# In the scan of a hybrid encoder block, ScalarE and VectorE keep the order of the program, and the splits of operands are spread over the background's pieces

## The chip, the cores and the metric

One core of a Trainium2 chip runs the kernel. The metric is the device time of one execution in microseconds (us); less is better. The kernel before takes 2295.72 us (median of three runs, 2294.54 to 2297.85).

Five engines work side by side, each on its own list of instructions: TensorE (PE in the profile; PEld is its loading of weights), VectorE (DVE), ScalarE (ACT), GpSimd (POOL) and SyncE (SP). Here SP issues nearly all the DMA transfers. An instruction that needs another engine's result waits for it, and what stands behind it on the same engine waits too.

## What is computed

The block takes 1024 tokens of width 1024 and 16 meta tokens. Everything is float32. Cut to what matters here:

```python
u = rmsnorm(hs) @ w_in                 # 1024 -> 9280: g_val, g_gate, z, xs, B, C, dt_f, dt_b, gate_conv, gate_ssm
y_conv = silu(layernorm(dwconv31(g_val * sigmoid(g_gate)))) @ conv_out_w
xs, B, C = silu(dwconv7(xs, B, C))
# SSD scan, chunks of 128, 4 groups of 8 heads, head width 64, state 128, both directions
y = ssd(xs, dt_f, a_f, B, C) + rev(ssd(rev(xs), rev(dt_b), a_b, rev(B), rev(C))) + d * xs
v = y * silu(z);  v = v * rsqrt(mean over each group of v * v) * ssm_norm_w
y_ssm = v @ ssm_out_w
hs = hs + (sigmoid(gate_conv) * y_conv + sigmoid(gate_ssm) * y_ssm) @ w_o
hs = hs + (silu(h @ w_gate) * (h @ w_up)) @ w_down        # h = rmsnorm(hs)
out = rmsnorm(hs)[:, 16:]
```

Inside a chunk the scan gives, for each head, a part from the chunk itself (a 128 x 128 matrix of decays times C B^T, applied to x), a part from the state that enters from the left, and a part from the state that enters from the right.

## The kernel before, in words

**Precision.** The large matmuls run on float32 numbers that are cut in two: a high part rounded to a shorter format (names ending in h) and the remainder (ending in l). A product is then three matmuls: high by high, high by low, low by high. So each operand has a *split*: one ScalarE instruction writes the high part, one VectorE or GpSimd instruction writes the remainder. Weights are split in `load_w`: SP loads half a block into `wraw` (two buffers), ScalarE casts it into `wh` (L138), VectorE or GpSimd subtracts into `wl` (L139).

**Stages.** Norm and projection of dt and z; projection of the rest with the two convolutions on VectorE; the *scan* (690 to 1265 us of the profile); then the output products, the merge, and the feed-forward part.

**The scan.** For each of four groups g there is first a backward pass (`backward(g)`, nine chunks from the right, three steps each: transpose x, transpose B, carry the state `s_b`, which is written to DRAM), and then a forward pass over eight chunks (class `Chunk`). The loop over 33 rounds does, in round f, parts of three chunks at once: loading and scores of the next one, outputs of the current one, norm and store of the last one, and up to six steps of the next group's backward pass. A string of letters is the order:

```python
SEQ = "LsDbS0NO5t3e4Pb7eT1VCeM62b"
```

L is `load` of the next chunk: TensorE forms C B^T in tile `cb`; VectorE masks it twice (`cb`, L777 and L778); `weigh` scales it by dt into `gg` (four ScalarE instructions, L788, then four of VectorE, L790); `split_small` splits C into `cch` and `ccl` (L691, L692). D is `outputs` of the current chunk: `split_over` splits the state from the right into `sbh` (ScalarE, L685) and, in place, `s_bl` (VectorE, L686); eight small matmuls `yd`; x times d (L834), added to yd (L835). b is a step of the backward pass. S and T are the scores: matmuls `ss`, exponential into `e` on ScalarE, times gg on VectorE. N, P and V belong to the last chunk: squares (L866), scaling by the norm (L870), transposes and store (L877, L878). O is `off_diag`: one matmul with the state from the left, and three with `sbh` and `s_bl`. C carries the state, M transposes and gates.

**The background.** Digits in the string are places at which pieces of other products are put in, to keep TensorE busy: `step_bg(n)` adds n to an account and runs one piece per whole unit, on average 3.3 pieces per round. A piece is six or nine matmuls of 128 x 512, and three pieces make an output, which ScalarE copies out of its PSUM bank (`w`, L553 for the gates, L656 for `s0`). In the chunk loop the pieces have one bank, `mm`. The background is eight blocks of gate weights (96 pieces) and then half of the product with ssm_out_w (`s0`, 48 pieces), whose moving operand is the normed rows of groups 0 and 1: `load_vn(0)` reads 16 tiles of 256 KB back from DRAM through `wraw` and splits them into `oph` and `opl` (L622, L623).

**Who sets the order.** The program's text gives every instruction a priority, and a scheduler lays out each engine's list with estimates of its own, so that an instruction may come ahead of others that were written earlier. For TensorE this is switched off in the scan: `tie` makes each matmul and transpose depend on the one written before it, without a semaphore, while `strict[0]` is true. ScalarE, VectorE, GpSimd and SP are laid out by the scheduler.

Of the kernel before, what the change touches and what calls it, by code (L numbers as in the profile page):

```python
# [8 lines left out]
F32 = mybir.dt.float32  # L9
F32R = mybir.dt.float32r  # L10
AF = mybir.ActivationFunctionType
ALU = mybir.AluOpType
# [3 lines left out]
P = 128  # L16
D = 1024
KC = D // P
# [39 lines left out]
def tile_hybrid_block(  # L58
# [4 lines left out]
    w_o, norm_ffn, w_gate, w_up, w_down, norm_final, out,  # L63
):
    nc = tc.nc
    V, S, GP, PE, SP = nc.vector, nc.scalar, nc.gpsimd, nc.tensor, nc.sync
    x = x[0]
    out = out[0]

# [2 lines left out]
    wts = ctx.enter_context(tc.tile_pool(name="wts", bufs=2))  # L72
# [13 lines left out]
    d_vn = [dram.tile([P, 4, T], F32, name=f"d_vn{g}") for g in range(G)]  # L86
# [34 lines left out]

    plan = []
    ready = []

    def load_w(view, lo):

        a, b = view.shape[1], view.shape[2]
        wh = wts.tile([P, 2048], F32R, name="wh", tag="wh")
        wl = wts.tile([P, 2048], F32R, name="wl", tag="wl")
        h3 = wh[:, : a * b].rearrange("p (a b) -> p a b", b=b)  # L130
        l3 = wl[:, : a * b].rearrange("p (a b) -> p a b", b=b)
        st = a // 2
        for i in range(2):
            raw = wts.tile([P, 1024], F32, name="wraw", tag="wraw", bufs=2)
            r3 = raw[:, : st * b].rearrange("p (a b) -> p a b", b=b)
            SP.dma_start(out=r3, in_=view[:, i * st:(i + 1) * st, :])
            sl = slice(i * st, (i + 1) * st)
            S.copy(out=h3[:, sl], in_=r3)  # L138
            (V if lo[i] == "v" else GP).tensor_tensor(out=l3[:, sl], in0=r3, in1=h3[:, sl].bitcast(F32), op=ALU.subtract)  # L139
        return h3, l3  # L140

    def next_w(key):

        while plan and len(ready) < 2:
            k, view, lo = plan.pop(0)
            ready.append((k, load_w(view, lo)))
        k, w = ready.pop(0)
        assert k == key, (k, key)
        return w
# [32 lines left out]
    plan_down(NFF // 2 - 1)  # L182

    last_mm = [None]
    strict = [False]

    def tie(mm):

        if strict[0]:
            tc.add_manual_dep(mm.ins, last_mm[0].ins.name,  # L190
                              mybir.DependencyInfo(mybir.DependencyClass.NoSync, mybir.DependencyReason.DATA),
                              reason="order")
        last_mm[0] = mm

    def matmul(out_, **kw):
        tie(PE.matmul(out_, **kw))  # L196

    def transpose(out_, in_, ident_):
        tie(PE.transpose(out_, in_, ident_))

    def mm3_parts(ps, wh, wl, oph, opl, parts):

        K = len(wh)
        for k in range(K):
            for i, (a, b) in enumerate(((wh[k], oph[k]), (wh[k], opl[k]), (wl[k], oph[k]))):
                matmul(ps, lhsT=a, rhs=b, start=(k == 0 and i == 0), stop=(k == K - 1 and i == 2))
            if k + 1 in parts:
                yield
# [8 lines left out]
    R_NM, R_NF, R_CB, R_LG, R_LB, R_SB, R_SN = 0, 8, 16, 24, 32, 40, 64  # L217
# [15 lines left out]
    def prm(r, i):  # L233
        return pr[:, r + i:r + i + 1]
# [369 lines left out]
    def op_tile():  # L604
        h = opp_box[0].tile([P, 512], F32R, name="oph", tag="oph")
        l = opp_box[0].tile([P, 512], F32R, name="opl", tag="opl")
        return h, l
# [4 lines left out]

    def load_vn(kh):

        op = []
        for hh in range(2):
            for k in range(KC):
                raw = wts.tile([P, 1024], F32, name="wraw", tag="wraw", bufs=2)[:, :512]
                SP.dma_start(out=raw, in_=d_vn[2 * kh + k // 4][:, k % 4, hh * 512:(hh + 1) * 512])
                h, l = op_tile()  # L620
                w = prm(R_SN, KC * kh + k)
                S.activation(out=h, in_=raw, func=AF.Copy, scale=w)  # L622
                V.scalar_tensor_tensor(out=l, in0=raw, scalar=w, in1=h.bitcast(F32), op0=ALU.mult, op1=ALU.subtract)  # L623
                op.append((h, l))
        return op

    def gemm(op, key, ps_of, parts=()):

        for b in range(4):
            wh, wl = next_w(f"{key}{b}")  # L630
            for hh in range(2):
                for j in range(2):
                    js = slice(j * P, (j + 1) * P)
                    ps = ps_of()
                    yield from mm3_parts(ps, [wh[:, k, js] for k in range(KC)], [wl[:, k, js] for k in range(KC)],
                                         [t[0] for t in op[hh * KC:(hh + 1) * KC]],
                                         [t[1] for t in op[hh * KC:(hh + 1) * KC]], parts)
                    yield 2 * b + j, hh, ps

    def background():  # L640
        for k, i in BGP:
            if k == "z":
                yield from z_block(i, sd, ps_bg, 2)
            else:
                yield from gate_block(k, i, d_gc if k == "gc" else d_gs, sd, ps_bg)
        hn_ctx.close()
        opp_box.append(ctx.enter_context(tc.tile_pool(name="ops", bufs=16, side="right")))
        op = load_vn(0)
        yield
        for done in gemm(op, "s0", ps_bg, PARTS):  # L650
            if done is None:
                yield
                continue
            i, hh, ps = done
            pt = sd.tile([P, 512], F32, name="w512", tag="w512", bufs=2)
            S.copy(out=pt, in_=ps)  # L656
            SP.dma_start(out=d_p[i, :, hh * 512:(hh + 1) * 512], in_=pt)
            yield

    ps_bg = lambda: pb(next(bg_ring[0]))  # L660
    bg = background()
    bg_acc = [0.0]
    strict[0] = True

    def step_bg(n):
        bg_acc[0] += n
        while bg_acc[0] >= 1:
            bg_acc[0] -= 1
            next(bg, None)

    def hbc(t, c, h0, nh, n, w):

        return t[:n, c, h0:h0 + nh].unsqueeze(2).broadcast_to([n, nh, w])
# [76 lines left out]
    class Chunk:  # L750


        def __init__(self, g, c):
            self.g, self.c = g, c
            self.hf, self.hb = g * HG, NH + g * HG
# [139 lines left out]
    for f in range(NCK + 1):  # L895
# [3 lines left out]
        if f % NTT == 0:  # L899
# [8 lines left out]
            V=lambda: old and old.store(), b=ahead, e=extra)  # L908
# [75 lines left out]
    def ln_split(hh):  # L984
        res = []
        for t in ln[hh][1]:
            o = op_tile()
            split(o, t, V)
            res.append(o)
        return res  # L990

    LN_STEPS = {1: (ln_load, 0), 2: (ln_center, 0), 3: (ln_load, 1), 4: (ln_center, 1), 5: (ln_stats, 0), 7: (ln_apply, 0), 9: (ln_stats, 1), 15: (ln_apply, 1)}
    op = load_vn(1)
    for n_, (i, hh, ps) in enumerate(gemm(op, "s1", pc)):
        ts = halves(hh)
        gt = gate(d_gs, i, ts)
# [6 lines left out]
    op = ln_split(0) + ln_split(1)  # L1003
# [44 lines left out]
    for b in range(4):  # L1048
        wh, wl = next_w(f"o{b}")
        for i in range(NTT):  # L1050
            ps = pc()
            sl = slice(i % 4 * P, (i % 4 + 1) * P)
# [130 lines left out]
```

## Time and profile before

| | us |
|---|---|
| median of three runs | 2295.72 |
| lowest and highest run | 2294.54, 2297.85 |
| the profiled execution's own time | 2297.74 |
| span of the profiled execution, first to last instruction | 2295.9 |
| TensorE busy in it | 2228.8 (97%) |
| granted clock of TensorE, mean | 0.991 of full speed |

The profiled execution is 2.0 us above the median. A line such as L138 is a line of the kernel above; the names left and right of `<-` are tiles. "Idle before" is the time in which the engine had nothing to run just ahead of an instruction, with the engine whose result ended it. The durations of merged rows (x4) run from the first start to the last end.

### The profile page before, as it was taken

To read this page: it belongs to the slowest core of one execution; us is meant where nothing else is said; L and a number is where in the kernel's file an instruction comes from. 1 tells how busy PE (TensorE), PEld (TensorE's weight loads), DVE (VectorE), ACT (ScalarE), POOL (GpSimd) and SP (SyncE) were. 2 spreads that over 40 slices of the span, in tenths; PEclk is the share of its full clock that TensorE was granted. 3 is DMA by queue.
4 is the path that set the end of the run, shared out by engine and by line. 5 is a ranking of instruction groups with operands and counts; after the bars stand their busy time and mean duration, and the time that the engine had idled before them with its cause. 6 is when DMAs were issued, how large, how long until landed. Compare 5 with 4: busy or idle time off the path is not lost.

```text
span 2295.9 us, 30987 instructions
## 1 busy us (share of the span) xinstructions
PE 2228.8 (97%) x12103; PEld 1903.6 (83%) x12103; DVE 1383.9 (60%) x1726; ACT 764.4 (33%) x1386; POOL 846.0 (37%) x729
## 2 busy tenths in 40 slices
PE   7999999999999999988999999999999999999998
PEld 7999999999997766665677788998888888888886
DVE  4389898997871587887997664533332333433236
ACT  6333342322322454545555462223111111111112
POOL 3374664821202586867785510111010110101102
PEclk9999999999999999999999999999999999999999
DMA  4222222232236675746753752411111111111111
GB/s 140 85 76 67 83 70 71 86 119 99 89 109 202 195 209 164 226 142 209 229 169 119 241 159 84 147 38 52 41 56 37 55 39 53 55 37 56 37 55 73
DMA packets 223162, 245.29 MB, mean 107 GB/s; under 512 B 19113, under 2 KB 174361, under 8 KB 223017
## 3 DMA queue, kind: packets, MB, share of 16 engines
q1 hardware_dynamic: 210200, 221.89, 31.3%
q10 hardware_dynamic: 12816, 21.44, 2.5%
q8 instruction: 95, 1.56, 0.3%
q14 instruction: 51, 0.41, 0.1%
HBM read 174.23 MB, written 69.04 MB: 106 GB/s over the span
## 4 chain that ended last, share of the span: by engine, by line
PE 48%; DMA 2%; DVE 2%; ACT 1%; POOL 1%; issue 1%; SPq 0%; POOLq 0%; DVEq 0%; ACTq 0%
PE yo L196 11%; PE mm L196 9%; PE ss L196 4%; PE yd L196 4%; PE cb L196 4%; PE yo L1107 3%; PE ss L1107 2%; PE cb L1107 2%; PE yd L1107 2%; DMA wraw<-d_vn 1%; PE mm L1107 1%; PE yo L1058 1%; PE cb L1058 1%; PE ss L1058 1%; PE mm L1058 1%
## 5 line engine op out<-in xcount | busy, mean ns | idle before, releaser
L139 POOL TENSOR_TENSOR wl<-wraw,wh 128x1024 fp32r<-128x1024 f32 (+1 forms) x103 | 249.9, 2436 | 1080.0 <-ACT wh L138 1079.8
L196 PE MATMUL mm<-hnh,wh 128*128 128x352 f32 (+4 forms) x1208 | 410.6, 340 | 14.9 <-ACT w L553 13.5
L196 PE MATMUL mm<-hnh,wl 128*128 128x352 f32 (+4 forms) x1208 | 403.8, 334 | 2.8 <-POOL wl L139 2.8
L196 PE MATMUL mm<-hnl,wh 128*128 128x352 f32 (+4 forms) x1208 | 405.8, 336 | 0.4 <-DVE hnl L378 0.4
L138 ACT CAST wh<-wraw 128x1024 fp32r<-128x1024 f32 (+1 forms) x172 | 175.0, 1042 | 420.3 <-PE yd L1107 175.5
L139 DVE TENSOR_TENSOR wl<-wraw,wh 128x1024 fp32r<-128x1024 f32 x69 | 139.2, 2020 | 252.6 <-ACT wh L138 247.8
L196 PEld LDWEIGHTS mm<-hnh,wh 128*128 128x128 f32 x1208 | 228.3, 189 | 29.9 <-ACT w L553 17.5
L474 DVE SCALAR_TENSOR_TENSOR acc<-ap,pr,acc 128x1024 f32<-128x1024 f32 x192 | 247.5, 1289 | 6.3
L196 PEld LDWEIGHTS mm<-hnh,wl 128*128 128x128 f32 x1208 | 228.3, 189 | 12.9 <-POOL wl L139 3.4
L196 PEld LDWEIGHTS mm<-hnl,wh 128*128 128x128 f32 x1208 | 228.2, 189 | 9.8 <-issue 1.2
L474 DVE SCALAR_TENSOR_TENSOR acc<-xp,pr,acc 128x1040 f32<-128x1040 f32 x120 | 156.6, 1305 | 4.0
L196 PE MATMUL mm<-oph,wh 128*128 128x512 f32 x344 | 139.5, 405 | 11.9 <-ACT w L656 9.9
L272 PE MATMUL mm<-wh,hnh 128*128 128x256 f32 x512 | 144.7, 283 | 5.1 <-ACT w L275 5.1
L272 PE MATMUL mm<-wl,hnh 128*128 128x256 f32 x512 | 144.6, 283 | 0.0
L272 PE MATMUL mm<-wh,hnl 128*128 128x256 f32 x512 | 144.5, 283 | 0.0
L196 PE MATMUL mm<-opl,wh 128*128 128x512 f32 x344 | 137.1, 398 | 3.0 <-DVE opl L623 3.0
L196 PE MATMUL yo<-oph,wh 128*128 128x512 f32 x352 | 139.0, 395 | 0.0
L196 PE MATMUL yo<-opl,wh 128*128 128x512 f32 x352 | 138.9, 395 | 0.0
L196 PE MATMUL yo<-oph,wl 128*128 128x512 f32 x352 | 138.8, 394 | 0.0
L196 PE MATMUL mm<-oph,wl 128*128 128x512 f32 x344 | 136.7, 397 | 0.0
L758 POOL TENSOR_SCALAR_AFFINE_SELECT sel<-adh 128x512 fp32r<-128x512 f32 x128 | 98.7, 792 | 70.8 <-ACT wh L138 41.6
L513 POOL TENSOR_TENSOR tap<-tap 128x1024 f32<-128x1024 f32 x40 | 96.1, 2403 | 34.4 <-ACT tap L509 33.3
(316 smaller groups left out, 4938.8 us busy)
## 6 DMA issues: line engine op xcount, KB each, us to landing
wraw<-in_w_in_dram SPq DMA_DIRECT2D x72, 512.0 KB, 3.7
xc<-d_x SPq DMA_DIRECT2D x64, 256.0 KB, 3.5
wraw<-in_w_gate_dram SPq DMA_DIRECT2D x22, 512.0 KB, 4.7
wraw<-in_w_up_dram SPq DMA_DIRECT2D x22, 512.0 KB, 3.8
wraw<-in_w_down_dram SPq DMA_DIRECT2D x22, 512.0 KB, 3.7
d_x<-xa ACTq DMA_DIRECT2D x16, 520.0 KB, 2.6
d_sz<-w ACTq DMA_DIRECT2D x64, 128.0 KB, 2.1
d_xt<-xt SPq DMA_DIRECT2D x32, 256.0 KB, 3.3
```

The lines of the kernel that those rows point to most:

```text
L138: S.copy(out=h3[:, sl], in_=r3)
L139: (V if lo[i] == "v" else GP).tensor_tensor(out=l3[:, sl], in0=r3, in1=h3[:, sl].bitcast(F32), op=ALU.subtract)
L196: tie(PE.matmul(out_, **kw))
L272: PE.matmul(ps[:, :256], lhsT=a[:, sl], rhs=bb[:, k, :], start=(k == 0 and q_ == 0), stop=(k == KC - 1 and q_ == 2))
L474: V.scalar_tensor_tensor(out=out_ if last else acc, in0=sl(k), scalar=w(k), in1=acc, op0=ALU.mult, op1=ALU.add)
L513: GP.tensor_tensor(out=t, in0=t, in1=part, op=ALU.add)
L758: GP.affine_select(out=dst, in_=hbc(src, self.c, h0, 4, P, P), pattern=[[0, 4], [-1 if back else 1, P]], compare_op=ALU.is_ge, fill=0.0, b ...
L1058: PE.matmul(ps[:, :256], lhsT=a[:, sl], rhs=bb[:, k, :], start=(k == 0 and q_ == 0), stop=(k == KC - 1 and q_ == 2))
L1107: PE.matmul(ps, lhsT=a[:, sl], rhs=bb[:, k, t0:t0 + n], start=(k == 0 and q_ == 0), stop=(k == 1 and q_ == 2))
```

## The change

A wrapper around VectorE and ScalarE does for them what `tie` does for TensorE: while `strict[0]` is true, each instruction that the program issues on the engine depends on the one that it issued before, so that the list keeps the order of the text. GpSimd and SP are still laid out by the scheduler. In the changed kernel every VectorE and ScalarE instruction has the wrapper's line, L85.

Two things are written in another place so that the text's order is one that can be kept. The splits of a weight block, which stood right behind its loads, are put into a list, `unsplit`, and are issued with the third and the fifth background piece after the loads (or, at the latest, ahead of the next block). The sixteen fills of `load_vn(0)`, which stood in one place, are issued three at a time, ahead of the first piece of `s0` and behind each further one; before each fill the pending weight splits are issued. The same code runs outside the scan with `strict[0]` false, and leaves everything there as it was.

```diff
-    V, S, GP, PE, SP = nc.vector, nc.scalar, nc.gpsimd, nc.tensor, nc.sync
+    strict = [False]
+
+    def follow(ins, last):
+
+        if strict[0] and last[0] is not None:
+            tc.add_manual_dep(ins.ins, last[0].ins.name,
+                              mybir.DependencyInfo(mybir.DependencyClass.NoSync, mybir.DependencyReason.DATA),
+                              reason="order")
+        last[0] = ins
+        return ins
+
+    class InOrder:
+
+
+        def __init__(self, eng):
+            self.eng, self.last = eng, [None]
+
+        def __getattr__(self, name):
+            op = getattr(self.eng, name)
+            return lambda *a, **k: follow(op(*a, **k), self.last)
+
+    V, S, GP, PE, SP = InOrder(nc.vector), InOrder(nc.scalar), nc.gpsimd, nc.tensor, nc.sync
...
-            sl = slice(i * st, (i + 1) * st)
-            S.copy(out=h3[:, sl], in_=r3)
-            (V if lo[i] == "v" else GP).tensor_tensor(out=l3[:, sl], in0=r3, in1=h3[:, sl].bitcast(F32), op=ALU.subtract)
+
+            def split_w(r3=r3, sl=slice(i * st, (i + 1) * st), eng=V if lo[i] == "v" else GP):
+                S.copy(out=h3[:, sl], in_=r3)
+                eng.tensor_tensor(out=l3[:, sl], in0=r3, in1=h3[:, sl].bitcast(F32), op=ALU.subtract)
+
+            if strict[0]:
+                unsplit.append([3 + 2 * i, split_w])
+            else:
+                split_w()
         return h3, l3
 
+    def split_due(n):
+
+        for e_ in unsplit:
+            e_[0] -= n
+        while unsplit and unsplit[0][0] <= 0:
+            unsplit.pop(0)[1]()
+
     def next_w(key):
 
+        split_due(1000)
         while plan and len(ready) < 2:
...
     def load_vn(kh):
 
-        op = []
+        op, fills = [], []
         for hh in range(2):
             for k in range(KC):
-                raw = wts.tile([P, 1024], F32, name="wraw", tag="wraw", bufs=2)[:, :512]
-                SP.dma_start(out=raw, in_=d_vn[2 * kh + k // 4][:, k % 4, hh * 512:(hh + 1) * 512])
-                h, l = op_tile()
...
+                def fill(hh=hh, k=k, i=len(op)):
+                    raw = wts.tile([P, 1024], F32, name="wraw", tag="wraw", bufs=2)[:, :512]
+                    SP.dma_start(out=raw, in_=d_vn[2 * kh + k // 4][:, k % 4, hh * 512:(hh + 1) * 512])
+                    h, l = op[i]
+                    w = prm(R_SN, KC * kh + k)
+                    S.activation(out=h, in_=raw, func=AF.Copy, scale=w)
+                    V.scalar_tensor_tensor(out=l, in0=raw, scalar=w, in1=h.bitcast(F32), op0=ALU.mult,
+                                           op1=ALU.subtract)
+
+                op.append(op_tile())
+                fills.append(fill)
+        return op, fills
...
-        op = load_vn(0)
+        op, fills = load_vn(0)
         yield
+
+        def fill3():
+            for _ in range(3):
+                if fills:
+                    split_due(1000)
+                    fills.pop(0)()
+
+        fill3()
         for done in gemm(op, "s0", ps_bg, PARTS):
+            fill3()
             if done is None:
                 yield
                 continue
...
             bg_acc[0] -= 1
             next(bg, None)
+            split_due(1)
```

**Place 1, VectorE, a round in the forward pass of group 0.** `cb_8310` is C B^T of the next chunk, `s_bl_8339` the state from the right of the current one, `ccl_8324` the remainder of C of the next. Before:

```order
L686 TENSOR_TENSOR s_bl_8339<-s_bl_8339,sbh_8343 128x512
L692 TENSOR_TENSOR ccl_8500<-cc_8484,cch_8499 128x128
L811 TENSOR_TENSOR e_8270<-e_8270,gg_8223 128x512
L703 TENSOR_TENSOR s_f_8283<-s_f_8283,yo_8281 128x512
L860 TENSOR_TENSOR y_8212<-tp_8286,y_8212 128x512
L861 TENSOR_TENSOR y_8212<-y_8212,sz_8167 128x512
L777 TENSOR_TENSOR cb_8310<-cb_8310,m_le_112 128x128
L834 TENSOR_TENSOR xc_8511<-xc_8511,dch_124 128x512
L778 TENSOR_TENSOR cb_8310<-cb_8310,m_ge_113 128x128
L835 TENSOR_TENSOR xc_8335<-yd_8346,xc_8335 128x512
L790 SCALAR_TENSOR_TENSOR gg_8314<-cb_8310,dt_151,gg_8314 128x128 x4
L843 TENSOR_TENSOR y_8382<-yo_8383,ea_154 128x512
```

Now, with the same tiles:

```order
L85 TENSOR_TENSOR s_f_8283<-s_f_8283,yo_8281 128x512
L85 TENSOR_TENSOR y_8212<-tp_8286,y_8212 128x512
L85 TENSOR_TENSOR y_8212<-y_8212,sz_8167 128x512
L85 TENSOR_TENSOR cb_8310<-cb_8310,m_le_112 128x128
L85 TENSOR_TENSOR cb_8310<-cb_8310,m_ge_113 128x128
L85 SCALAR_TENSOR_TENSOR gg_8314<-cb_8310,dt_151,gg_8314 128x128 x4
L85 TENSOR_TENSOR ccl_8324<-cc_8308,cch_8323 128x128
L85 TENSOR_TENSOR s_bl_8339<-s_bl_8339,sbh_8343 128x512
L85 TENSOR_TENSOR xc_8335<-xc_8335,dch_124 128x512
L85 TENSOR_TENSOR xc_8335<-yd_8346,xc_8335 128x512
L85 TENSOR_TENSOR e_8374<-e_8374,gg_8314 128x512
L85 TENSOR_TENSOR y_8382<-yo_8383,ea_154 128x512
```

The split `s_bl_8339` stood in the round before its own, six instructions ahead of `cb_8310`; now it stands behind both masks of `cb_8310`, the four `gg_8314` and `ccl_8324`. The split of C stood a round early as well (`ccl_8500` is the round after's). TensorE's list is the same in both; on it `cb_8310` comes ahead of the matmuls with `s_bl_8339`.

**Place 2, ScalarE, where the fills of `load_vn(0)` begin.** `oph` are the fills' high parts, `y_10379` is the last chunk's rows (letter P), `e_10586` and `e_10712` (or `e_10752`) exponentials. Before:

```order
L622 ACTIVATE oph_10628<-wraw_10626,pr_123 128x512
L622 ACTIVATE oph_10634<-wraw_10632,pr_123 128x512
L870 ACTIVATE y_10379<-y_10379,rs_10590 128x512
L720 COPY xt_10578<-tp_10573 128x512
L788 ACTIVATE gg_10526<-cb_10522,dt_151 128x128 x4
L810 ACTIVATE e_10586<-ss_10581 128x512
L685 CAST sbh_10831<-s_bl_10827 128x512
L622 ACTIVATE oph_10640<-wraw_10638,pr_123 128x512
L788 ACTIVATE gg_10605<-cb_10522,dt_151 128x128 x4
L622 ACTIVATE oph_10646<-wraw_10644,pr_123 128x512
L726 COPY bt_10742<-tp_10740 128x128
L810 ACTIVATE e_10752<-ss_10747 128x512
```

Now:

```order
L85 ACTIVATE gg_10605<-cb_10522,dt_151 128x128 x4
L85 ACTIVATE oph_10626<-wraw_10658,pr_123 128x512
L85 ACTIVATE oph_10628<-wraw_10662,pr_123 128x512
L85 ACTIVATE oph_10630<-wraw_10666,pr_123 128x512
L85 CAST wh_10670<-wraw_10672 128x1024
L85 CAST wh_10670<-wraw_10674 128x1024
L85 ACTIVATE oph_10632<-wraw_10687,pr_123 128x512
L85 ACTIVATE oph_10634<-wraw_10691,pr_123 128x512
L85 ACTIVATE oph_10636<-wraw_10695,pr_123 128x512
L85 ACTIVATE y_10379<-y_10379,rs_10590 128x512
L85 COPY bt_10702<-tp_10700 128x128
L85 ACTIVATE e_10712<-ss_10707 128x512
```

Fills stood one or two at a time between other work, and the next weight block was split behind all of them; now six fills and the two casts of the next block of ssm_out_w stand in one row ahead of the scaling of `y_10379`, whose transposes TensorE does in the same round. VectorE's list has the matching eight instructions in one row.

## Rows read from the trace of the kernel before

**Rows 1.** Part 1 of the page: busy us, share of the span, instructions.

```profile
PE 2228.8 (97%) x12103; PEld 1903.6 (83%) x12103; DVE 1383.9 (60%) x1726; ACT 764.4 (33%) x1386; POOL 846.0 (37%) x729
```

**Rows 2.** Stretches: us and busy PE, PEld, DVE, ACT, POOL; PEclk, DMA share, GB/s.

```profile
690.00:770.00 80.00, 78.46 (x362) 61.14 (x361) 16.10 (x22) 22.68 (x46) 19.68 (x19) 1.00 0.66 204
770.00:1265.00 495.00, 461.15 (x2348) 337.54 (x2347) 403.57 (x719) 257.39 (x633) 367.39 (x443) 0.98 0.62 184
```

**Rows 3.** TensorE's waits, 690 to 1310 us: us in total, times, longest.

```profile
PE mm L196 <- ACT w L553: 13.5, 11, 3.2
PE mm L196 <- ACT w L656: 9.9, 7, 3.1
PE mm L196 <- DVE opl L623: 3.0, 3, 1.4
PE yd L196 <- DVE e L811: 2.2, 2, 2.0
PE mm L196 <- ACT oph L622: 2.0, 1, 2.0
...
PE yo L196 <- DVE s_b L703: 1.1, 1, 1.1
```

**Rows 4.** Timeline of TensorE, one chunk: start, us, line, out<-in, shapes [idle before <-releaser].

```profile
960.89 1.02 PE L196 MATMUL yo<-xw,bt 128*128 128x512 f32 x2
961.75 0.38 PE L196 MATMUL cb<-cc,bc 128*128 128x128 f32 x2
...
963.09 0.66 PE L199 MATMUL tp<-ident,xc 128*128 128x128 f32 x4
963.50 0.48 PE L196 MATMUL ss<-sel,u_gt 128*128 128x512 f32 x1
...
965.60 0.39 PE L196 MATMUL yo<-s_bl,cch 128*128 128x512 f32 x1
```

**Rows 5.** Timeline of VectorE, 886 to 920 us, same columns.

```profile
888.36 1.13 DVE L790 SCALAR_TENSOR_TENSOR gg<-cb,dt,gg 128x128 f32<-128x128 f32 x4 [1.31 <-ACT gg L788]
889.40 0.68 DVE L843 TENSOR_TENSOR y<-yo,ea 128x512 f32<-128x512 f32 x1
...
915.91 0.69 DVE L703 TENSOR_TENSOR s_b<-s_b,yo 128x512 f32<-128x512 f32 x1 [1.24 <-PE yo L196]
916.52 0.29 DVE L777 TENSOR_TENSOR cb<-cb,m_le 128x128 f32<-128x128 f32 x1
916.85 0.30 DVE L778 TENSOR_TENSOR cb<-cb,m_ge 128x128 f32<-128x128 f32 x1
```

**Rows 6.** Timeline of ScalarE, same stretch.

```profile
887.20 1.12 ACT L788 ACTIVATE gg<-cb,dt 128x128 f32<-128x128 f32 x4
```

**Rows 7.** Single lines of VectorE: ns min/median/max, over the whole run.

```profile
L686 DVE TENSOR_TENSOR s_bl<-s_bl,sbh x28: 676/968/1779, 762.5 to 1229.1; 128x512 fp32r<-128x512 f32 x28
...
L692 DVE TENSOR_TENSOR ccl<-cc,cch x32: 275/714/1375, 709.4 to 1216.4; 128x128 fp32r<-128x128 f32 x32
```

**Rows 8.** Timeline of TensorE at two waits for an emptied bank.

```profile
1016.62 0.50 PE L196 MATMUL mm<-hnh,wh 128*128 128x512 f32 x1 [3.23 <-ACT w L553]
...
1269.20 0.50 PE L196 MATMUL mm<-oph,wh 128*128 128x512 f32 x1 [0.49 <-ACT w L656]
```

**Rows 9.** Busy time by stretch, after the first of these waits.

```profile
1016.60:1024.00 7.40, 7.38 (x30) 6.01 (x30) 3.21 (x7) 1.87 (x4) 2.40 (x4) 0.77 0.22 61
```

**Rows 10.** Instructions and loads of tile wraw, 1040 to 1125 us.

```profile
L622 ACT ACTIVATE oph<-wraw,pr x16: 706/722/751, 1060.1 to 1106.2; 128x512 fp32r<-128x512 f32 x16
L623 DVE SCALAR_TENSOR_TENSOR opl<-wraw,pr,oph x16: 735/752/1764, 1060.9 to 1107.6; 128x512 fp32r<-128x512 f32 x16
...
L138 ACT CAST wh<-wraw x2: 1050/1052/1055, 1109.6 to 1112.9; 128x1024 fp32r<-128x1024 f32 x2
L139 DVE TENSOR_TENSOR wl<-wraw,wh x2: 1648/1856/2064, 1111.0 to 1114.2; 128x1024 fp32r<-128x1024 f32 x2
...
DMA to landing us min/median/max: 3.3/3.5/4.6
```

More of the change, by code (lines that the diff above doesn't have):

```diff
@@ L123, in tile_hybrid_block @@
     ready = []
+    unsplit = []
     def load_w(view, lo):
@@ L184, in tile_hybrid_block @@
     last_mm = [None]
[L185 to L193, printed above, removed]
     def matmul(out_, **kw):
-        tie(PE.matmul(out_, **kw))
+        follow(PE.matmul(out_, **kw), last_mm)
     def transpose(out_, in_, ident_):
-        tie(PE.transpose(out_, in_, ident_))
+        follow(PE.transpose(out_, in_, ident_), last_mm)
     def mm3_parts(ps, wh, wl, oph, opl, parts):
@@ L613, in load_vn @@
     def load_vn(kh):
-        op = []
+        op, fills = [], []
         for hh in range(2):
             for k in range(KC):
-                raw = wts.tile([P, 1024], F32, name="wraw", tag="wraw", bufs=2)[:, :512]
-                SP.dma_start(out=raw, in_=d_vn[2 * kh + k // 4][:, k % 4, hh * 512:(hh + 1) * 512])
-                h, l = op_tile()
[L621 to L625, printed above, removed]
+                def fill(hh=hh, k=k, i=len(op)):
[9 more added lines that the diff above has]
+        return op, fills
     def gemm(op, key, ps_of, parts=()):
@@ L992, in tile_hybrid_block @@
     LN_STEPS = {1: (ln_load, 0), 2: (ln_center, 0), 3: (ln_load, 1), 4: (ln_center, 1), 5: (ln_stats, 0), 7: (ln_apply, 0), 9: (ln_stats, 1), 15: (ln_apply, 1)}
-    op = load_vn(1)
+    op, fills = load_vn(1)
+    for fill in fills:
+        fill()
     for n_, (i, hh, ps) in enumerate(gemm(op, "s1", pc)):
```

## The prediction

> **What bounds the kernel now.** Part 1 of the page first: TensorE is busy for 97% of the span, VectorE for 60%, ScalarE for 33% [rows 1]. That is a mean over unlike stages, so I went to the busy time by stretch [rows 2]. In the chunk loop TensorE runs 461.15 of 495 us and VectorE 403.57, or 82%: TensorE sets the pace and idles for 34 us, and VectorE has 18% of slack, where the whole span gives it 40%. In that slack an order without choice must find room. TensorE's waits in the scan say what the idle time is [rows 3]: 13.5 and 9.9 us, 23.4 in 18 waits, are for a background bank that ScalarE had not yet emptied (`w`); 5.0 us are for the fills (`opl`, `oph`); 2.2 us are for `e`. Nearly nothing is for the states: 1.1 us, once. The granted clock is 0.98 in the chunk loop and 1.00 in the backward pass ahead of it [rows 2], so the lower clock takes about 0.02 x 495 = 10 us.
>
> So the most that the change can win in the scan is near 34 + 10 us, and what it can lose is every chain that used to start early. The order of the text has three such places.
>
> **Term 1, the state from the right.** Before, `s_bl` was split in the round before its own. Now VectorE does it behind both masks of the next chunk's `cb`, its four `gg` and `ccl` (place 1). TensorE's own schedule runs `cb` at 961.75 and wants `s_bl` at 965.60, 3.85 us later [rows 4]. I build the chain on that chunk. A backward step comes just ahead: the matmul of its state starts at 960.89 and takes 1.02 [rows 4], so `s_b` can start at about 961.95. From its start to that of the first mask are 0.61 us, from there 0.33 to the second, and 0.30 for that [rows 5]: ScalarE has the masked `cb` at 963.19. It needs 1.12 us for four `gg` [rows 6]; VectorE starts its own four when the last of them is done (887.20 + 1.12 = 888.32, start 888.36) and its next instruction follows 1.04 us later [rows 5, 6]. With 0.04 us for each hand-over that is 963.23, 964.35, 964.39, 965.43. Then `ccl`, 0.71 at the median, and `s_bl`, 0.97 [rows 7]: 967.1 against 965.60, **a wait of 1.5 us**. At the shortest `ccl` and `s_bl` (0.28 and 0.68) it is 0.8; at the longest (1.38 and 1.78) 3.0. Without a backward step in front the first mask starts at 962.17 and not 962.56: 1.1 us. In the last group there is no backward step at all, and TensorE has no transposes of `xc` between `cb` and `s_bl` either, 0.41 us less (963.09 to 963.50) [rows 4]: 1.1 + 0.4 = 1.5 us.
>
> There are 28 rounds with an `s_bl` [rows 7]: by the lists 15 with a backward step in front, 6 without, 7 in the last group. In three of them, one of each kind, a background piece stands between the scores and the state's matmuls and covers the wait. That leaves 14 x 1.5 + 5 x 1.1 + 6 x 1.5 = **35.5 us**. From 18 us (0.8, 0.4 and 0.8 at the minima) to 62 (every round at 3.0, less some that catch up).
>
> The rows of `s_bl` spread from 676 to 1779 ns for one shape [rows 7], so something that does not stand in VectorE's list stretches it. The Trainium skill ("SBUF — State Buffer", section "Who interferes with whom") says that a VectorE instruction with two inputs in SBUF contends with a GpSimd instruction that reads SBUF, and that whoever starts first keeps the other out for its whole length. By it `ccl` and `s_bl`, both of that form, would sit out a GpSimd instruction more often where they stand amid the masks than where they stood, and the term would lie towards its 62 us end, the time towards 2338 + 26 = 2364. The spread agrees with a block of this kind, but no row here shows which instruction blocked; I keep the medians.
>
> **Term 2, weight splits ahead of the masks.** In four rounds a `wl` of 1.86 us [rows 10] now stands right ahead of the masks, one of them a round without `s_bl`. Where TensorE's own matmuls ahead of `cb` don't cover it, the chain starts up to 1.9 us later. I take **3 us** (0 to 8).
>
> **Term 3, the fills.** Six fills, with the next block's two `wh` and `wl` between, now stand in one row on both engines, ahead of the scaling of `y` (place 2), whose transposes TensorE wants about 3.2 us after the first `opl` starts. They share two buffers of `wraw`, so a load starts only when the remainder ahead of it is done. Counting from that first `opl`, with 3.5 us from issue to landing (4.6 for a weight half), `oph` 0.72, `opl` 0.75, `wh` 1.05 and `wl` 1.86 [rows 10]: `opl` of fills 0 and 1 end at 0.75 and 1.5; fill 2 is loaded from 0.8, split by 5.8; the first half of the weights, loaded from 1.5, has its `wl` at 9.0; the second, from 5.8, at 13.3; fill 3, loaded from 9.0, has its `opl` at 14.0; fill 4, loaded from 13.3, has its `oph` at 17.5, its `opl` at 18.3; fill 5, loaded from 14.0, has its `oph` at 18.2. Then `y` is scaled, by 18.9. The transposes wait 18.9 - 3.2 = 15.7 us; the first matmuls on `opl` 0 and 1 wait some 1.7 before that. In the next round the masks stand behind fills 6 to 8, which makes that round's wait 5.9 and not 1.5, 4.4 more. Fills 9 to 14 come in neighbouring pieces ahead of one more `y`: 5.4 for a `w` copy behind them and 3.3 for the transposes, 8.7. Together 17.4 + 4.4 + 8.7 = **30.5 us**, against 5.0 before [rows 3], which goes. If loads land in 3.3 us and part of the chain runs ahead of TensorE it is 17; at 4.6 for every load, about 35.
>
> **Term 4, the copies out of the bank.** Each `w` now stands right behind its piece, not behind whatever the scheduler put first. The 23.4 us of 18 waits [rows 3] fall to what the copy itself costs: nine times, by the lists, the first piece of an output follows the last of another directly, and such a wait is 0.49 us [rows 8]. 9 x 0.5 = 4.5, a gain of **18.9 us** (10 to 23). The 2.2 us for `e` go too: 2.0.
>
> **What costs nothing.** No instruction is added, and TensorE's list in the scan is unchanged. GpSimd's and SP's lists shift by a few places; GpSimd runs 367 of 495 us [rows 2] and its results (`xw`, `sel`) cost TensorE almost nothing now. If that cover went, an `xw` late by one GpSimd instruction would cost a round well under 1 us, which I leave to the range.
>
> **The clock.** After the 3.23 us wait [rows 8] the granted clock is 0.77 over 7.4 us [rows 9], 1.7 us lost. Waits of that size go (Term 4) and others come (Term 3), the many new ones are half as long; I take the loss as unchanged, 0.
>
> **Sum.** 35.5 + 3 + 30.5 - 5 - 18.9 - 2 = +43.1 against the profiled execution's 2297.74 us: 2340.8. That execution lies 2.0 us above the runs' median, so the runs should show **2338 us**, 1.9% slower. The terms' own ends give 18 + 0 + 17 - 5 - 23 - 2 = +5 and 62 + 8 + 35 - 5 - 10 - 2 = +88, which don't all fall together.
>
> **The rivals.**
> *Faster.* The chain of Term 1 fits into TensorE's 3.85 us, and the fills overlap, because TensorE is held up elsewhere in the round, or VectorE runs ahead. It decides by one comparison: `s_bl` done within 3.85 us of `cb`. For it speaks that VectorE is idle 18% of the loop; against it that with a backward step the chain is 0.8 us too long even with the shortest rows. Then only the gains stay, 5 + 18.9 + 2 = 26, and a few us of clock with them: 2295.7 - 26 = 2270. Chance 0.15.
> *Only the fills cost.* The chain hides, the blocks of fills don't: 30.5 - 5 - 18.9 - 2 = +4.6, 2300. Chance 0.12.
> *The clock falls with the new waits.* If each of the 25 new waits is followed by a stretch as after the wait of 3.23 us, 25 x 1.7 = 43 us come on top: 2381. For it speaks that the 0.77 followed a wait [rows 8, 9]; against it that those waits were twice as long. The Trainium skill ("TensorE: Matmul & The Clock Gate", section "A second HAM failure mode: psum-queue depth-cycling") describes a kernel in which frequent short idling of TensorE between groups of matmuls makes the clock swing between its two levels; by that page the time would be this rival's 2381. Chance 0.13.
> *No effect.* If the lists did not change, nothing would; both places show that they do. Chance near 0.
>
> The forecast has the remaining 0.60, with cases in which the fills overlap and only the chain costs (2296 + 38.5 - 26 = 2308) inside it. **Range: 2298 to 2380**, which leaves out the faster rival and the end of the clock's. A measurement of this kernel tells 0.2%, 4.6 us, from no change. Faster by more: 0.15, the first rival. Within it: 0.09, most of the second and the low end of the forecast. Slower: 0.76.
>
> **What would show it.** In the changed kernel's waits of TensorE: a new row `yo` for `s_bl`, 20 to 28 times, 1 to 2 us each; one wait of over 10 us of a transpose for `y` with `oph` ahead of it on ScalarE; the rows for `w` down to a few us in all; TensorE's busy time in the loop unchanged, and the granted clock still near 0.98. No row for `s_bl` would prove the first term wrong; a clock of 0.9 in the loop, the last rival right.

## The result, and the profile after

The changed kernel takes **2355.82 us** (median of 4 runs, 2353.36 to 2358.08) against 2295.69 for the kernel before in the same comparison: ratio 1.0261, interval 1.0243 to 1.0278. It is slower by 60 us; the forecast was slower by 42, with 2355.8 inside the range. The two profiled executions differ by 57.1 us of span (2353.0 against 2295.9), and the accounts below are made against that.

The page's first part and the busy time by stretch (columns as in [rows 2]) of the changed kernel. The chunk loop ends at about 1317 us now, so that the stretch holds the same 2348 matmuls:

```profile
PE 2236.4 (95%) x12103; PEld 1903.0 (81%) x12103; DVE 1375.5 (58%) x1726; ACT 760.4 (32%) x1386; POOL 844.0 (36%) x729
```

```profile
770.00:1317.00 547.00, 469.49 (x2348) 338.81 (x2347) 396.97 (x723) 254.59 (x637) 367.60 (x443) 0.96 0.56 166
```

The loop took 495 us before and takes 547: 52 of the 57. TensorE's idle time in it went from 33.9 to 77.5 us (+43.7), and the same matmuls are busy 8.3 us longer, at a granted clock of 0.96 against 0.98 [rows 2]. The other 5 us are lost after the scan. TensorE's waits from 690 to 1366 us say where (total, times, longest; every ScalarE and VectorE instruction has the wrapper's line, so the tile tells them apart):

```profile
PE yo L223 <- DVE s_bl L85: 24.8, 21, 1.5
PE tp L226 <- ACT y L85: 18.7, 9, 11.9
PE mm L223 <- ACT w L85: 14.7, 16, 5.5
PE yo L223 <- ACT sbh L85: 5.8, 5, 2.8
PE tp L226 <- DMA xc<-d_x: 5.1, 1, 5.1
PE yo L223 <- DVE s_f L85: 4.5, 3, 2.7
PE mm L223 <- DVE opl L85: 4.2, 1, 4.2
PE yo L223 <- DVE wl L85: 2.4, 1, 2.4
```

The two chains that the prediction built are on top: the split of the state, 21 times 1.2 us, and one wait of 11.9 us for `y`. The waits for `w` fell, from 23.4 us [rows 3] to 14.7. Three rows were not foreseen: `xc`, `s_f` and, after the scan, `wl`.

**The chain of the state, in one round.** TensorE, then VectorE, then ScalarE (start, us, line, operation, tiles, shapes, idle before):

```profile
980.41 0.50 PE L223 MATMUL yo<-sbh,cch 128*128 128x512 f32 x1 [0.56 <-ACT sbh L85]
982.10 0.50 PE L223 MATMUL yo<-s_bl,cch 128*128 128x512 f32 x1 [1.19 <-DVE s_bl L85]
```

```profile
977.86 0.28 DVE L85 TENSOR_TENSOR cb<-cb,m_le 128x128 f32<-128x128 f32 x1
978.18 0.30 DVE L85 TENSOR_TENSOR cb<-cb,m_ge 128x128 f32<-128x128 f32 x1
979.69 1.13 DVE L85 SCALAR_TENSOR_TENSOR gg<-cb,dt,gg 128x128 f32<-128x128 f32 x4 [1.21 <-ACT gg L85]
980.73 0.28 DVE L85 TENSOR_TENSOR ccl<-cc,cch 128x128 fp32r<-128x128 f32 x1
980.93 1.12 DVE L85 TENSOR_TENSOR s_bl<-s_bl,sbh 128x512 fp32r<-128x512 f32 x1
```

```profile
978.51 1.14 ACT L85 ACTIVATE gg<-cb,dt 128x128 f32<-128x128 f32 x4 [4.21 <-DVE cb L85]
```

From the start of the first mask to the start of `ccl` the prediction had 962.56 to 965.43, 2.87 us; in this round it is 977.86 to 980.73, 2.87. The steps are as forecast: ScalarE's four `gg` wait for the second mask, VectorE's four for the last of ScalarE's, and VectorE stands idle for 1.21 us between with `s_bl` behind it.

**The block of fills.** TensorE at its three waits, and ScalarE's own row ahead of `y` (same columns):

```profile
1078.28 0.50 PE L223 MATMUL mm<-oph,wh 128*128 128x512 f32 x1 [0.57 <-ACT oph L85]
...
1082.96 0.80 PE L223 MATMUL mm<-opl,wh 128*128 128x512 f32 x1 [4.19 <-DVE opl L85]
...
1098.78 1.12 PE L226 MATMUL tp<-ident,y 128*128 128x128 f32 x4 [11.89 <-ACT y L85]
```

```profile
1085.72 0.72 ACT L85 ACTIVATE oph<-wraw,pr 128x512 fp32r<-128x512 f32 x1 [6.88 <-DMA wraw<-d_vn]
1088.11 1.04 ACT L85 CAST wh<-wraw 128x1024 fp32r<-128x1024 f32 x1 [1.67 <-DMA wraw<-in_ssm_out_w_dram]
1090.84 1.04 ACT L85 CAST wh<-wraw 128x1024 fp32r<-128x1024 f32 x1 [1.68 <-DMA wraw<-in_ssm_out_w_dram]
1093.22 0.72 ACT L85 ACTIVATE oph<-wraw,pr 128x512 fp32r<-128x512 f32 x1 [1.34 <-DMA wraw<-d_vn]
1095.78 0.72 ACT L85 ACTIVATE oph<-wraw,pr 128x512 fp32r<-128x512 f32 x1 [1.84 <-DMA wraw<-d_vn]
1097.40 0.72 ACT L85 ACTIVATE oph<-wraw,pr 128x512 fp32r<-128x512 f32 x1 [0.90 <-DMA wraw<-d_vn]
1098.02 0.70 ACT L85 ACTIVATE y<-y,rs 128x512 f32<-128x512 f32 x1
```

Every bracket in ScalarE's row names a load into `wraw`: the engine waits for data six times in 12 us while `y` stands behind. The stretch around it:

```profile
1078.00:1106.00 28.00, 11.64 (x36) 7.94 (x36) 15.25 (x23) 9.00 (x14) 7.49 (x9) 0.63 0.49 150
```

TensorE works for 11.64 of 28 us, and the granted clock is 0.63: most of that stretch is at the lower of its two levels.

### The profile page after: what moved, and what is told of

It reads as the page before. It is cut to its first block, busy times and chain, and to the rows that moved or that the text cites. A ratio compares the mean times of both kernels' runs of the same rounds, so it can differ in the third digit from the quotient of the medians.

```text
span 2353.0 us, 31008 instructions
## 1 busy us (share of the span) xinstructions
PE 2236.4 (95%) x12103; PEld 1903.0 (81%) x12103; DVE 1375.5 (58%) x1726; ACT 760.4 (32%) x1386; POOL 844.0 (36%) x729
## 4 chain that ended last, share of the span: by engine, by line
PE 79%; DVE 6%; POOL 4%; DMA 3%; issue 3%; ACT 2%; SPq 0%; POOLq 0%; DVEq 0%; ACTq 0%
PE mm L223 32%; PE yo L223 13%; PE ss L223 6%; PE mm L299 5%; PE yd L223 5%; PE cb L223 4%; PE yo L1150 3%; POOL tap L540 2%; PE ss L1150 2%; PE cb L1150 2%; PE yd L1150 2%; PE tp L226 2%; DMA wraw<-d_vn 1%; PE mm L1150 1%; PE yo L1101 1%
## 5 line engine op out<-in xcount | busy, mean ns | idle before, releaser
L85 ACT CAST wh<-wraw 128x1024 fp32r<-128x1024 f32 (+1 forms) x172 | 175.0, 1042 | 412.2 <-PE yd L1150 175.5
L85 DVE TENSOR_TENSOR wl<-wraw,wh 128x1024 fp32r<-128x1024 f32 x69 | 136.5, 1978 | 280.6 <-ACT wh L85 280.6
L85 DVE SCALAR_TENSOR_TENSOR acc<-ap,pr,acc 128x1024 f32<-128x1024 f32 x192 | 247.5, 1289 | 6.3
L85 DVE SCALAR_TENSOR_TENSOR acc<-xp,pr,acc 128x1040 f32<-128x1040 f32 x120 | 156.6, 1305 | 4.0
L799 POOL TENSOR_SCALAR_AFFINE_SELECT sel<-adh 128x512 fp32r<-128x512 f32 x128 | 87.5, 704 | 124.0 <-PE ss L223 82.3
```

Of the source, the lines that this page charges most:

```text
L85: return lambda *a, **k: follow(op(*a, **k), self.last)
L799: GP.affine_select(out=dst, in_=hbc(src, self.c, h0, 4, P, P), pattern=[[0, 4], [-1 if back else 1, P]], compare_op=ALU.is_ge, fill=0.0, b ...
```

## The experiments

All kernels below start from the changed one unless said otherwise. Ratios are to the kernel before.

**1. The state's split ahead of the masks.** A new method, called at the start of the round, loads and splits the current chunk's state; `outputs` does so no more.

```diff
+        def early(self):
...
+                SP.dma_start(out=s_bl, in_=d_sb[g][c])
+                self.s_bl = split_over(s_bl)
...
+        if cur:
+            cur.early()
         for k in SEQ:
```

> The changed kernel with one thing moved: the load and split of s_bl of the current chunk are written at the start of the round, ahead of the next chunk's masks; both engines still keep the order of the text. Theory (the place of s_bl behind the masks, gg and ccl makes TensorE wait): the waits of yo for s_bl (24.8 us) and sbh (5.8 us) go, the masks start about 1 us later, which the scores hide: about 2325 us (2318 to 2332). Rival (VectorE has no room in the round, so an order without choice costs the same wherever s_bl stands): the wait turns up at the masks' users, e, yd or y, and the time stays over 2345.

Measured 2335.72 us, 1.016 (1.0145 to 1.0175): 20 us less, between the two. The waits for `s_bl` and `sbh` went as the theory says, but TensorE's waits now read (in the experiments they are those of the whole execution, unless said otherwise; over it the changed kernel's row for `w` is 15.2 us in 17 waits, longest 5.5):

```profile
PE mm L223 <- ACT w L85: 21.7, 17, 10.7
PE tp L226 <- ACT y L85: 20.6, 9, 11.6
PE yo L223 <- DVE s_f L85: 9.6, 4, 3.9
...
PE yo L223 <- DVE y L85: 3.7, 1, 3.7
...
PE yo L223 <- DVE s_bl L85: 0.5, 1, 0.5
```

30.1 us went (24.8 + 5.8, less the 0.5 left), and the 5.1 us for `xc` with them; 5.1 came back at `s_f`, 5.2 at a `w` that stands behind fills, 3.1 at `y` on VectorE, 1.9 at `y` on ScalarE. The cause is shown; 15.3 of the 35.2 us reappeared at what stands next.

**2. Fills without the two buffers.** Each fill is loaded into its own `opl` tile, one piece ahead, and split in place.

```diff
-                    raw = wts.tile([P, 1024], F32, name="wraw", tag="wraw", bufs=2)[:, :512]
+                    raw = l.bitcast(F32)
...
-                    split_due(1000)
```

> The changed kernel with one thing else: the fills of load_vn(0) no longer go through the two wraw buffers; each is loaded straight into its opl tile and split in place, loads a piece ahead of the splits; the pending weight splits are no longer forced between them. Theory (the block of fills costs because each load waits for a wraw buffer): the wait of the transposes for y falls from 11.9 to about 2 us, that for opl from 4.2 to under 1, the copy of w behind the fills from 5.5 to under 1, sbh from 2.8 to about 0: some 21 us less, 2335 us (2328 to 2341). Rival (six to nine fills in one row are too much work for ScalarE and VectorE themselves): the wait for y stays over 6 us and the time over 2345.

Measured 2333.08 us, 1.0152 (1.0137 to 1.0167): 23 us less, as the theory has it. Its waits:

```profile
PE yo L223 <- DVE s_bl L85: 24.6, 21, 1.5
PE mm L223 <- ACT w L85: 10.1, 17, 0.8
PE yo L223 <- ACT sbh L85: 8.4, 6, 4.9
...
PE tp L226 <- ACT y L85: 5.0, 8, 1.6
...
PE mm L223 <- DVE opl L85: 4.2, 1, 4.2
```

The wait of 11.9 us is gone, that for `w` behind the fills too (longest 0.8 after 5.5). Two parts of the theory were wrong. `opl` still costs 4.2, so that wait does not come from the buffers. And the longest wait for `sbh` was to go from 2.8 to about 0; it rose to 4.9. The edit does three things at once (no shared buffers, loads a piece ahead, no weight splits forced between the fills); how much each of them gives was not tested apart.

**3. Both together.**

> Both of these edits together. Theory, with the two causes independent: about 2304 us (2296 to 2312), some 10 us over the kernel before, or under it if TensorE's clock comes back with the waits (TensorE's busy time is 7.6 us longer in the changed kernel than before: then 2297). Rival (the order without choice is what costs, in other places as soon as these are mended): over 2325.

Measured 2312.09 us, 1.0061 (1.0046 to 1.0076). The two gains add up (20.1 + 22.7 = 42.8, measured 43.7): two separate causes. The time lies just past the upper end of what was expected, and 14.7 us over the kernel before are left.

**4. The text alone, without the order.** `V` and `S` are the engines themselves, the spread splits and fills stay.

> The changed kernel without the wrapper: ScalarE and VectorE are laid out by the scheduler again, while the splits of weights and the fills stay spread over the pieces. Theory (the order costs, the spreading itself does not): s_bl is split a round early again, no wait for it, fills stand between other work, 2290 to 2305 us. Rival (it is the spreading through two wraw buffers that costs): the waits for opl, oph and y stay near 15 us and the time is over 2312.

Measured 2301.21 us, 1.0015 (1.0005 to 1.0024). The spreading itself costs 3 to 4 us (1 to 5.5 by the interval); the rest of the 60 comes only with the order. There is no row for `s_bl` and none for `y`. The fills still cost more than before, 8.1 us for `oph` and 2.3 for `opl` against 5.0 together [rows 3], which is what the rival named, at two thirds of its size. The waits for `w` are nearly as before:

```profile
PE mm L223 <- ACT w L580: 13.9, 11, 3.2
PE mm L223 <- ACT w L696: 8.3, 7, 2.3
```

**5. and 6. One engine in order, the other not.** The wrapper on ScalarE alone, then on VectorE alone.

> The changed kernel with the wrapper on ScalarE alone; VectorE is laid out by the scheduler. Theory (s_bl needs sbh of ScalarE, opl needs oph, and gg goes from one engine to the other, so either list alone fixes the chain): waits for s_bl and sbh over 20 us together, the wait for y near 10 us, 2330 to 2352 us. Rival (it is VectorE's list alone that costs): under 2312 us, no row for s_bl.

> The changed kernel with the wrapper on VectorE alone; ScalarE is laid out by the scheduler. Theory: as with ScalarE alone, s_bl stands behind the masks, gg and ccl on VectorE: wait for s_bl near 25 us, that for the fills near what it was, and the copies w late again: 2335 to 2358 us. Rival (it is ScalarE's list alone that costs): under 2312 us.

Measured 2368.34 (1.0304, 1.0283 to 1.0325) and 2396.86 us (1.0428, 1.0411 to 1.0446). Either alone is enough, as the theory says, but both are slower than its range, and than both engines in order. TensorE's waits with ScalarE alone, and then with VectorE alone, where 25 us were expected for `s_bl`:

```profile
PE yo L223 <- DVE s_bl L727: 32.2, 24, 3.2
...
PE yo L223 <- ACT sbh L85: 12.5, 13, 1.8
```

```profile
PE yo L223 <- DVE s_bl L85: 56.5, 22, 4.1
```

With VectorE alone in order, one round shows how (VectorE, then ScalarE):

```profile
1014.74 1.12 DVE L85 SCALAR_TENSOR_TENSOR gg<-cb,dt,gg 128x128 f32<-128x128 f32 x4 [3.10 <-ACT gg L829]
```

```profile
1012.95 0.72 ACT L911 ACTIVATE y<-y,rs 128x512 f32<-128x512 f32 x1 [1.70 <-POOL rs L140]
1013.58 1.12 ACT L829 ACTIVATE gg<-cb,dt 128x128 f32<-128x128 f32 x4
```

The scheduler put the scaling of `y`, which waits for GpSimd, ahead of ScalarE's `gg`. VectorE, which may not do anything else, waits 3.10 us where it waited 1.21, and `s_bl` with it.

The waits are not all of it. TensorE is busy for 2258.0 us in run 5 and 2254.5 in run 6, against 2236.4 with both engines in order, for the same 12103 matmuls; its granted clock is 0.93 in run 5's loop (770 to 1330 us) and 0.92 in run 6 (770 to 1345 us), against 0.96. In run 5 TensorE idles no longer than in the changed kernel (2374.4 - 2258.0 = 116.4 us of the span, against 2353.0 - 2236.4 = 116.6): what its profiled execution, the slowest of its four, takes more is all busy time at the lower clock. In run 6 both are longer, idle time by 21.6 us and busy time by 18.1.

**7. and 8. What was left, place by place.** Both edits of run 3; the first state of a group made in `early`; `w` copied ahead of the fills of the same piece; two fills of the first piece through `wraw` with the empty piece, then one, two, three and two a piece. In the second, ScalarE and VectorE are free at the scan's last background pieces.

```diff
+            if self.first:
+                self.first()
...
             S.copy(out=pt, in_=ps)
...
+            fill3()
```

> Both edits of the combined run, and three more: the first state of a group (s_f) is made at the start of the round, ahead of the masks; the copy w stands ahead of the fills that follow the same piece; the fills start one piece earlier, two of them through wraw, and go two a piece after the first eight. Theory (what is left in the combined run is again single places where something stands in front of what TensorE needs next): the waits for s_f (9.6 us) go, those for oph and opl (6.1 us) and w behind the fills (1.6 us) go for the most part: 12 to 16 us less than the combined run's 2312, 2296 to 2301. Rival (each place mended opens another one of the same size): 2307 or more.

> As the mended kernel; the end of the scan's last background pieces is laid out by the scheduler for ScalarE and VectorE. The lists of ScalarE come out the same, so theory and rival both say: the same time as the mended kernel within 3 us; it shows how far two builds with nearly one order differ.

Measured 2303.13 (1.0019, 1.0009 to 1.0028) and 2300.94 us (1.001, 0.9999 to 1.0021): the second differs from the first by no more than was expected, and from the kernel before by nothing that can be told. The first is 9 us under run 3, where 12 to 16 were expected: `s_f` left the table, the 2.3 and 3.8 us for `oph` and `opl` stayed, and VectorE's `y` and `s_b` rose from 3.8 and 2.2 us to 6.5 and 3.6. The time is neither theory's nor rival's.

**9. and 10. Fills earlier, and the tail.** The first two fills right behind the last gate piece; in the second run the fills of `load_vn(1)` go straight into their `opl` tiles too.

> The mended kernel with the free tail, and the first two fills written still earlier, right behind the last gate piece, ahead of the masks and both lots of gg of that round. Theory (oph and opl of the first piece are late because eight gg stand in front of them on both engines: 2.3 and 3.8 us in that run): these two waits go, about 5 us less than 2301: 2294 to 2298. Rival (the splits only push s_b, s_bl and the masks of that round back by as much): 2300 or more.

> The same, and the fills of load_vn(1), after the scan, are loaded straight into their opl tiles too. Theory (the tail's waits for w, oph, opl and wl, some 7 us, come from wraw, which is handed on late by the deferred split of the last weight block): 5 to 7 us less than the run with the earlier fills: 2288 to 2292, under the kernel before, 0.2 to 0.4% by ratio. Rival (the opl tiles come free too late, since each has to wait for its last matmul of the first half): the same as the other run or slower.

Measured 2301.04 (1.0017, 1.0008 to 1.0026): a miss for the theory, and the rival's number, though not in the places that it named. The first matmuls on `oph` and `opl` wait no longer, and the same round loses most of the time again, at `y`. TensorE reaches its transposes sooner; the scaling comes behind three more fills (ScalarE, 1060.76 to 1062.76 us) and then waits 1.36 us for GpSimd's factor:

```profile
1064.89 1.11 PE L227 MATMUL tp<-ident,y 128*128 128x128 f32 x4 [4.30 <-ACT y L86]
```

```profile
1064.12 0.72 ACT L86 ACTIVATE y<-y,rs 128x512 f32<-128x512 f32 x1 [1.36 <-POOL rs L141]
```

The second measured 2294.79 us, 0.9988 (0.9980 to 0.9997): 6 us less than run 9 for the tail, as expected in size, though not down to the 2288 to 2292 us forecast. It is **the only version whose median lies under the kernel before**, by 0.12%: its interval leaves out 1 by little, and 0.12% is less than the 0.2% set ahead as what can be told.

**11. and 12. The scaling of `y` ahead of the fills.** In the changed kernel, then in the version of run 10:

```diff
-SEQ = "LsDbS0NO5t3e4Pb7eT1VCeM62b"
+SEQ = "LsDbS0NO5tP3e4b7eT1VCeM62b"
```

> The changed kernel with one letter moved in the string of the round: P, the scaling of y on ScalarE, right behind t, ahead of the background pieces 3 and 4 and so ahead of the fills and of the casts of weights that come with them. Theory (y waited only because it stands behind them; the fills themselves stay slow, through two wraw buffers): the 18.7 us of waits for y fall to about 2, and some 6 us come back where the second piece of s0 then waits for fills 3 and 4 (opl, oph): about 2345 us (2340 to 2348). Rival (the fills cost nothing by themselves once y is out of their way): 2339 or less, waits for oph and opl as they were.

> The run with fills and tail mended, and P moved in the same way. There the waits for y are 12.5 us in nine places, behind fills or casts of weights. Theory: most of them go and nothing takes their place, since its fills don't wait for wraw: 2283 to 2289 us, 0.4 to 0.6% under the kernel before. Rival (ScalarE then waits for the norm's factor of GpSimd ahead of the fills, and passes the wait on to e, oph and gg): 2293 or more.

Measured 2361.4 (1.0276, 1.0262 to 1.0291) and 2309.81 us (1.0058, 1.0045 to 1.0071): neither is faster for the edit. Run 12 is slower than run 10 by 0.7%; run 11's interval overlaps the changed kernel's (1.0243 to 1.0278), so its 0.15% more can't be told from no change. Run 11 is neither theory's number; run 12 is on the rival's side. In run 11 TensorE's long wait for `y` (11.9 us) went, nearly whole, to the next in ScalarE's list behind the fills, the copy `bt`:

```profile
PE tp L226 <- ACT bt L85: 10.2, 1, 10.2
...
PE tp L226 <- ACT y L85: 2.1, 1, 2.1
```

And ScalarE, asked for `y` sooner, now waits for GpSimd's factor with everything behind it; its own waits in that run, and below them the same row of the changed kernel (770 to 1300 us there, 770 to 1317 here):

```profile
ACT y L85 <- POOL rs L140: 50.8, 27, 3.8
```

```profile
ACT y L85 <- POOL rs L140: 12.8, 6, 3.8
```

That is the mechanism that the rival of run 12 names. There TensorE's wait is not passed on to `e`, `oph` and `gg`, as it said, but to `w`: from 13.5 us in run 10 to 23.5.

## Why the prediction was right, and where it was short

Direction and mechanism were right: slower, by the chain of the state and by the fills, in the places named. The size was 18 us short (2338 against 2355.8; its own sum, less the 2.0 us, gives 2338.8). Term by term, from the two traces:

- **Term 1** (35.5): 24.8 + 5.8, less the 2.8 of one `sbh` that belongs to the fills: 27.8. Taken away, in run 1, the waits vanish. In the round shown the chain up to `ccl` takes what was forecast to 0.01 us; 21 rounds wait where 25 were counted, 1.2 us each where 1.4 was the mean. Term 2 (3) can't be told apart from it; no run isolates it.
- **Term 3** (30.5): 0.57 + 4.19 + 11.89 = 16.7 for the first round (17.4), 2.77 + 0.75, less an ordinary 1.2, = 2.3 for the second (4.4), 5.54 + 1.84 = 7.4 for the third (8.7): 26.4. That the first round comes so close is luck: two errors offset. The transposes waited 11.9 us, not 15.7, as the loads landed in 2.7 us, not 3.5, the `wl` took 1.23, not 1.86, and TensorE came to them 4.9 us after the first `opl` began, not 3.2; the first matmuls on `oph` and `opl` waited 4.8 us, not 1.7. The changed kernel's tile `wraw`, 1040 to 1160 us (ns min/median/max):

```profile
L85 DVE TENSOR_TENSOR wl<-wraw,wh x2: 1225/1226/1227, 1089.2 to 1091.9; 128x1024 fp32r<-128x1024 f32 x2
...
DMA to landing us min/median/max: 2.6/2.7/2.8
```

  The 4.2 us for `opl` do not come from the buffers: run 2 has them still, and run 9, with the first fills ahead of the round's `gg`, does not.
- **Term 4** (18.9): `w` without the 5.5 behind the fills is 9.2 us, a gain of 14.2. The copy stands right behind its piece, as said, but TensorE meets it 15 times and not nine, mostly at 0.56 to 0.67 us. The gain for `e` (2.0) and for the old `opl` and `oph` (5.0) came.
- **The clock** (0): this is the term that failed most. What the long waits for `w` cost was to go and other waits were to bring as much. The first came: around the 3.23 us wait of before (974.5 to 1021.3 us; here 991.5 to 1031.1) the same matmuls are busy 3.6 us less. But around the fills (1061.4 to 1117.3; here 1073.2 to 1154.7) they are busy 6.2 us longer, around the 5.1 us wait for `xc` 1.7, and in the loop 8.3 in all. It was not the rival's way either: the 21 waits of about 1.2 us for `s_bl` did not drag the clock down. With five of them in it, the loop's start is granted 1.00; the stretch of the fills 0.79, and 0.91 before (columns as in [rows 2]):

```profile
770.00:920.00 150.00, 136.45 (x698) 98.20 (x697) 115.27 (x212) 72.90 (x187) 112.99 (x134) 1.00 0.60 175
```

```profile
1073.20:1154.70 81.50, 50.59 (x204) 34.84 (x204) 48.59 (x82) 33.77 (x75) 38.78 (x46) 0.79 0.58 173
```

  The page that the rival named, "TensorE: Matmul & The Clock Gate" of the Trainium skill (section "A second HAM failure mode: psum-queue depth-cycling"), has a clock that swings with frequent short idling. The changed kernel's trace does not show that at this size; the clocks of 0.93 and 0.92 in the loops of runs 5 and 6, where more or longer waits for the state stand in the rounds, fit it.
- **What was not in the sum**: `xc` 5.1, `s_f` 4.5, the rest of the waits for `y` 5.0, and 5 us after the scan: 19.6 together. "What costs nothing" was the step that missed them. Two of them are one mechanism that the prediction used only at two places: in a list without choice, whatever comes behind a late instruction is late. The split of the last weight block, deferred by five pieces, gives `wraw` back late, and the fills after the scan start behind it; run 10 shows it. `s_f` of a group's first chunk stands behind the same masks and `gg` as `s_bl`, and went in run 7, when it too was put ahead of them. The other waits for `y` look alike, but no run takes them apart. The 5.1 us for `xc`, a load that SP issued late once, went in run 1; which order on SP caused it stays open.

The sum of what was measured is 27.8 + 26.4 - 14.2 - 2.0 - 5.0 + 8.3 + 19.6 = 60.9; four small rows of before that are gone too (`bt`, `s_b`, `e` and `sel` ahead of TensorE, 4.0 us) bring it to 56.9, against 57.1. That the forecast is only 14 us off this (43.1) owes something to luck: Terms 1 to 3 were 14.8 us too large together (69.0 against 54.2), and what it lacked or had too good (the clock, the rows that were not in the sum, 4.7 of the gain for `w`) comes to 32.6.

Of the rivals: "faster" fell with the first row of the waits. "Only the fills cost" is what run 1 built, and it lies at 1.016, not at the 2300 us of that rival: `w`, `s_f` and `y` took 15.3 us back, and the rest is not worked out here.

## What to carry to other kernels

Before the change one engine kept an order by hand and the others had a choice. Each engine that is fixed as well needs its own order worked out, by asking for every instruction that another engine waits for how late the one ahead of it can be. A hand-over back and forth (mask, `gg` on one engine, `gg` on the other) is a place where nothing should stand behind that somebody else needs soon; loads through a buffer that is handed on are another. Removing one such wait moves part of it to the next in the list, so count what comes back (two fifths in run 1, all of it in run 11). Fixing one of two coupled engines was worse here than fixing both, in part by TensorE's clock.

## What the runs showed of the hardware

`s_bl` has two durations in the changed kernel. VectorE's instruction on that tile (ns min/median/max), then GpSimd's timeline in the round shown above:

```profile
L85 DVE TENSOR_TENSOR s_bl<-s_bl,sbh x28: 680/1114/1121, 780.5 to 1290.4; 128x512 fp32r<-128x512 f32 x28
```

```profile
980.19 1.32 POOL L799 TENSOR_SCALAR_AFFINE_SELECT sel<-adl 128x512 fp32r<-128x512 f32 x2
```

In all 23 cases of about 1.11 us a `sel` of GpSimd was running when it started, and ended 0.56 to 0.58 us later (in the round above the second of these two, which end at 981.51); in the three cases of 0.68 us with nothing of that kind beside it, none was. The one of 0.98 us started beside an `xw` that ended 0.43 us later. Once, at 1112.7, it started within 0.01 us of an `xw` of GpSimd and took 0.68 us, and the `xw` took 1.59, where the shortest takes 1.03. That fits the Trainium skill's "SBUF — State Buffer", section "Who interferes with whom": a VectorE instruction with two inputs in SBUF and a GpSimd instruction that reads SBUF exclude each other, and who starts first goes first. By that page the prediction put the term towards 62 us; the trace shows the block, 0.43 us of it at 23 of the 28 `s_bl`, and the term still came out under its middle: fewer rounds wait, and in the round shown `ccl` and `s_bl` together take 1.32 us (980.73 to 982.05), where 1.68 were taken, as `ccl` is short (475 ns at the median over the run, where 714 was taken [rows 7]). Which instruction blocked before, the prediction left open. The trace of before shows it: at the start of 24 of its 28 `s_bl` a GpSimd instruction was running, 19 times `y<-y,y`, else an `xw`, a `sel` or an `s_f`; at the start of the other four, of 676 to 693 ns, none was. In run 1, with `s_bl` ahead of the masks, its median is 688 ns.
